# Neighbourhood attention layer on one core: where the sums of the output weights are formed, and in which order the first three row pairs are multiplied

## The chip, the cores and the metric

The kernel runs on one core of a Trainium2 chip. Its time is the device time of one execution in microseconds, and a kernel's number is the median of its runs. A trace comes from one further execution under the hardware profiler; it has its own time, which is given beside the span that the trace covers.

A core has five engines with a queue of instructions each, worked off in order: TensorE (PE; its weight loads are shown apart as PEld), VectorE (DVE), ScalarE (ACT), GpSimd (POOL) and SyncE (SP). They wait for each other through semaphores alone. SyncE issues almost all DMAs here. A DMA takes one of eight lanes in turn, and its issue waits until the DMA before it on the same lane, that is the eighth before it, has landed.

## The reference

One layer, in float32, on 2048 tokens of width 1024, seen as a grid of 32 rows by 64 columns with 16 heads of 64:

```python
def neighbourhood_mixer(h, w_in, rpb):
    B, S, _ = h.shape
    proj = h @ w_in
    q, k, v, gate = jnp.split(proj, 4, axis=-1)
    heads = lambda a: a.reshape(B, S, N_HEADS, HEAD_DIM)
    o = neighbourhood_attention(heads(q), heads(k), heads(v), rpb)
    return o.reshape(B, S, D_INNER), gate

def reference(x, norm_0, w_in_0, rpb_0, w_out_0, norm_1, w_in_1, w_out_1, norm_f):
    layers = ((norm_0, w_in_0, rpb_0, w_out_0), (norm_1, w_in_1, None, w_out_1))
    for i in range(DEPTH):
        g, w_in, rpb, w_out = layers[i]
        h = rmsnorm(x, g)
...
            o, gate = neighbourhood_mixer(h, w_in, rpb)
...
        x = x + (o * jax.nn.silu(gate)) @ w_out
    return rmsnorm(x, norm_f)
```

`DEPTH` is 1. Each query attends to a window of 8 rows by 16 columns with a bias per head. The part that the change touches is the last product, `(o * silu(gate)) @ w_out`, with `w_out` of 1024 x 1024, and the residual and the norm behind it.

## The kernel before, in words

**Precision.** Every large product is made in a format of reduced precision (fp32r). A float32 operand is split into a high part (a copy by ACT) and a low part (DVE subtracts the high part from the operand), and a product is three matmuls: high by high, low by high, high by low. `split_to` (L508 on) and `form_rows` (L1408) do this.

**Seven products.** Two halves in each of the three dimensions would take eight block products; a scheme with sums takes seven. At the end of the kernel one such unit is a pair of row tiles of 128 tokens. The left operand A is the gated attention output of the pair (A11, A12 of the first tile, A21, A22 of the second), the right one, B, is `w_out` in four quarters B11, B12, B21, B22 of 512 x 512, each four blocks of 128 x 512 with an index k. The products are P1 = A11 B11, P2 = A12 B21, P3 = S4 B22, P4 = A22 T4, P5 = S1 T1, P6 = S2 T2, P7 = S3 T3. S1 to S4 are sums of A (`sum_rows`), and the sums of B are T1 = B12 - B11, T3 = B22 - B12, T2 = B22 - T1 and T4 = B21 - T2; each is written over one of its operands, T1 over B11, T3 over B12, T2 over B22 and T4 over B21. A product is 12 matmuls of 128 x 128 by 128 x 512: four k by three of the split. P2 adds into the bank of P1 after P1's result was copied (`p1`, by ACT), P7 and P4 into that of P6, P3 into that of P5.

**Stages.** `stage_one` (to about 322 us) makes 12 units of the input projection and half of the values by seven products. `stage_two` (L799) finishes V: `pair(u, ts, ...)` (L889 to L902) multiplies V tiles of 24 or 48 matmuls, and puts a step of other work (its later arguments) behind every quarter of them. These steps make V's eviction (`v`, ACT, L392, and its store, L395), load and split V's weights (`lw`, L531, and `w`, L540 and L543), form the sums of the inputs (`t123`, `t4`, L863 to L871) and split them (`form`, `t1`, L518 and L519), and form the first operands of the projections that follow (`ahead`, L418, L419, sums L425). Then `run` makes these projections; the first product starts at 411.30 us in the trace. There the copy of P1 is L444, and P2 is its third product.

**Attention.** 32 cycles follow, one for each pair of heads and quarter of the rows, with scores (L1028), a softmax whose normalising of `x` is shared by DVE, ACT and GpSimd (L1054, L1056), transposes (`ph`, L1113), copies of these by DVE and ACT (`pta`, L1089) and values (`o`, L1135). Projections, and later the plain output products of the first six row tiles (L1337 to L1341), are fed between. The gated output goes to DRAM (`ogd`, L1144).

**The end.** `rows_by_seven` (L1465) multiplies the other ten row tiles as five pairs. The quarters of `w_out` are loaded in the last two cycles (`land_first`, 11 blocks; `land_rest`, 5 blocks), GpSimd forms T1 (`sum_T1`, L1374) and T2 and T3 (`sums_T23`, L1378 and L1379), DVE forms T4 (`sum_T4`, L1383), and `split_quarter` (L1394 by ACT, L1395 by DVE) splits all 16 blocks into the places that have come free by then. B11, B21 and B22 themselves lie split in `woh` and `wol` from the plain output products. The order of the products (`seq`) is P1 of the first three pairs, P2 of the first three pairs, and then 6, 7, 5, 4, 3 of the first pair, of the second and of the third, and after that each of the last two pairs in the order 1, 6, 2, 7, 5, 4, 3. `todo` hangs the other steps on places of this list: a product's operand is formed three products ahead (`form_rows`), and the loads and sums of rows and the residual's loads stand at fixed distances.

**Order.** Nothing is scheduled by a program: every engine works in the order in which the code calls it. `store(key, lag, f)` puts a DMA on a list, and `due(n)` issues what has become due after `lag` further matmuls; the DMA still takes its place in SyncE's one queue, and waits there for its data and its lane while everything behind it waits too.

Of the kernel before, what the change touches and what calls it, by code (L numbers as in the profile page):

```python
# [32 lines left out]
PLAIN = 6  # L33
# [38 lines left out]
def build(ctx, tc, x, xr, xt, wg, rpb, last, w_out, n0, nf, masks, out):  # L72
# [7 lines left out]
    ogd = [dram.tile([128, 4, NP, 128], F32, name=f"ogd{T}") for T in range(4)]  # L80

# [75 lines left out]
    woh, wol = {}, {}  # L157

# [640 lines left out]
    def stage_two():  # L799
# [81 lines left out]

        def t1(*ks):
            def g():
                for k in ks:
                    split_to(*X2["B12"][k], x12[k], None)
                X2["T1"] = X2["B12"]
            return g

        pair(0, (8, 9), both(w(0, 3), lambda: spread_rstd(3)), both(lw(1, 0), block("B12", x12, 0, 1)), block("B12", x12, 2, 3),  # L889
             block("B22", x22, 0, 1))  # L890
        pair(0, (10, 11), both(v(0, 8, 9), block("B22", x22, 2, 3)), t123(0), t123(1), lw(1, 1))
        pair(0, (12, 13), v(0, 10, 11), t123(2), t123(3), both(t4(0, 1, 2, 3), lw(1, 2)))
        pair(0, (14, 15), both(v(0, 12, 13), w(1, 0)), both(w(1, 1), lw(1, 3)), w(1, 2), w(1, 3))
        pair(1, (12,), v(0, 14, 15), form("T2", x11, 0), form("T2", x11, 1))
        pair(1, (13,), both(v(1, 12), form("T2", x11, 2)), form("T2", x11, 3))
        pair(1, (14,), both(v(1, 13), form("T3", x22, 0)), form("T3", x22, 1))
        pair(1, (15,), both(v(1, 14), lambda: ahead(-9, -1)), form("T3", x22, 2), form("T3", x22, 3))
        pair(1, (8,), both(v(1, 15), lambda: ahead(-8, -1)), t1(0), t1(1), lambda: ahead(-7, -1))
        pair(1, (9,), both(v(1, 8), t1(2)), t1(3), lambda: ahead(-6, -1), form("T4", x21, 0))
        pair(1, (10,), both(v(1, 9), form("T4", x21, 1)), form("T4", x21, 2), form("T4", x21, 3))  # L900
        pair(1, (11,), both(v(1, 10), lambda: ahead(-5)), lambda: ahead(-4), both(lambda: ahead(-3), lambda: ahead(-2)),
             both(lambda: ahead(-1), v(1, 11)))  # L902
# [451 lines left out]
    quarters = {"B11": (0, 0), "B12": (0, 1), "B21": (1, 0), "B22": (1, 1)}  # L1354

    def load_quarter(f, k, to):
        r, c = quarters[f]
        R[f, k] = to
        nc.sync.dma_start(to, w_out[(4 * r + k) * 128:(4 * r + k + 1) * 128, c * 512:c * 512 + 512])

    def land_first():
        spot = mkp([128, 3, 512], F32, "land")
        homes = [spot[:, i] for i in range(3)] + [kp([128, 960], F32, "land")[:, :512]]
        homes += [mp([128, 512], F32, "land") for _ in range(4)] + [p([128, 512], F32, "land") for p in (qp, sp, lp)]
        which = [(f, k) for f in ("B12", "B11") for k in range(4)] + [("B22", k) for k in range(3)]
        return [lambda w=w, h=h: load_quarter(*w, h) for w, h in zip(which, homes)]

    def land_rest():
        for w in [("B22", 3)] + [("B21", k) for k in range(4)]:
            load_quarter(*w, mp([128, 512], F32, "land"))  # L1370

    def sum_T1():
        for k in range(4):
            nc.gpsimd.tensor_tensor(R["B11", k], R["B12", k], R["B11", k], OP.subtract)  # L1374

    def sums_T23(ks):
        for k in ks:
            nc.gpsimd.tensor_tensor(R["B12", k], R["B22", k], R["B12", k], OP.subtract)  # L1378
            nc.gpsimd.tensor_tensor(R["B22", k], R["B22", k], R["B11", k], OP.subtract)  # L1379

    def sum_T4():
        for k in range(4):
            nc.vector.tensor_tensor(R["B21", k], R["B21", k], R["B22", k], OP.subtract)  # L1383

# [3 lines left out]
    def split_quarter(f, homes):  # L1388
        src = {"T1": "B11", "T2": "B22", "T3": "B12", "T4": "B21"}[f]
        TF[f] = []  # L1390
        for k in range(4):
            h, l = homes.pop(0), homes.pop(0)
            t, h, l = R[src, k], h() if callable(h) else h, l() if callable(l) else l
            nc.scalar.activation(h, t, AF.Copy)  # L1394
            nc.vector.tensor_tensor(l, t, h.bitcast(F32), OP.subtract)  # L1395
            TF[f].append((h, l))

    def fresh(p, n=512):
        return lambda: p([128, n], F32R, "t")[:, :512]

    def load_rows_of(m, f):
# [3 lines left out]
        A[m, f] = raw([128, 512], F32, "raw")  # L1405
# [59 lines left out]
    def rows_by_seven():  # L1465
        for f, (r, c) in plain_of.items():
            TF[f] = [(woh[4 * r + k, c], wol[4 * r + k, c]) for k in range(4)]
        E = 3 if PLAIN <= 6 else 2
        seq = [(m, P) for P in (1, 2) for m in range(E)] + [(m, P) for m in range(E) for P in order7 if P not in (1, 2)]
        seq += [(m, P) for m in range(E, len(PAIRS)) for P in order7]  # L1470
        at = {s: i for i, s in enumerate(seq)}
# [4 lines left out]

        for i, s in enumerate(seq):
            if i >= 2 * E:
                on(i - 3, form_rows, *s)
        for m in range(len(PAIRS)):  # L1480
            s = at[m, 6] - (m >= E)
            loads = {0: (), 1: ((-7, "A21"), (-6, "A22")), 2: ((-7, "A21"), (-6, "A22"), (-6, "A11"), (-6, "A12"))}
            for d, f in loads.get(m, ((-7, "A21"), (-7, "A22"), (-6, "A11"), (-4, "A12"))):
                on(s + d, load_rows_of, m, f)
# [5 lines left out]
        for f in ("A21", "A22"):  # L1490
            load_rows_of(0, f)
# [217 lines left out]
```

## Time and profile before

| | us |
|---|---|
| runs, median (lowest, highest) | 1065.47 (1064.48, 1067.84) |
| profiled execution, its own time | 1068.24 |
| span of its trace | 1066.5 |
| TensorE busy in the span | 1044.3 |

| stretch | what runs |
|---|---|
| 0 to 322 | stage one |
| 324 to 411 | V tiles of stage two |
| 411 to 936 | projections, attention, plain output products |
| 936 to 948 | transposes and values of the last cycle |
| 948 to 1060 | 35 products of the five pairs |
| 1060 to 1066.5 | last row's norm and store |

The trace is read in views: the page (busy time of each engine, groups of instructions), windows (busy time of each engine in a stretch), waits (which engine waited for which instruction: total, times, longest), the timeline (start, duration, engine, line, names of tiles, number of instructions run together; in brackets the idle time before it and what ended it), and the chain of waits that ended last. L12 is line 12 of the kernel before. A number such as 128x512 is partitions by elements of a tile.

### The profile page before, as it was taken

The page shows a single profiled execution, that of the slowest core. Times are in us where ns is not written, and L with a number is a line of the kernel's source. Part 1 is how long each engine was busy: PE and PEld are TensorE (multiplying, and loading weights), DVE is VectorE, ACT ScalarE, POOL GpSimd, SP SyncE. Part 2 cuts the span into 40 slices and gives each one's busy share as a digit, 9 for nine tenths or more (in the row PEclk, how much of TensorE's full clock was granted, in tenths as well). Part 3 has the DMA queues.
Part 4 walks back from the last instruction along what each step waited for, and adds up shares of the span by engine and source line. Part 5 has one row for each costly group of instructions (what it writes and reads, how often), then busy time and mean ns, then how long its engine had stood idle before and what let it go on. Part 6 is the DMA issues. An engine that isn't in the chain of part 4 may idle for free.

```text
span 1066.5 us, 20216 instructions
## 1 busy us (share of the span) xinstructions
PE 1044.3 (98%) x7256; PEld 852.9 (80%) x7256; DVE 742.4 (70%) x1589; ACT 558.4 (52%) x1305; POOL 297.4 (28%) x369
## 2 busy tenths in 40 slices
PE   9999999999999999999999999999999999988897
PEld 6888888887888888888888788888877778866686
DVE  5476657778897635465655766678787887778886
ACT  7645233533344334232333677788888777744333
POOL 0000322312221000000002576656556223361231
PEclk9999999999999999999999999999999999988999
DMA  9634444444545334333326878788885798964452
GB/s 315 218 99 121 131 143 138 126 132 142 174 135 148 113 89 108 109 102 121 103 89 226 246 224 246 208 249 272 242 262 186 221 333 258 323 212 126 141 178 80
DMA packets 124285, 189.05 MB, mean 177 GB/s; under 512 B 11224, under 2 KB 55512, under 8 KB 124184
## 3 DMA queue, kind: packets, MB, share of 16 engines
q1 hardware_dynamic: 123752, 187.35, 56.1%
q8 instruction: 57, 0.93, 0.3%
q10 hardware_dynamic: 432, 0.40, 0.1%
q14 instruction: 44, 0.36, 0.1%
HBM read 137.38 MB, written 50.33 MB: 176 GB/s over the span
## 4 chain that ended last, share of the span: by engine, by line
PE 87%; DVE 6%; DMA 2%; ACT 2%; issue 1%; POOL 1%; SPq 0%; ACTq 0%; DVEq 0%; POOLq 0%
PE pp L436 36%; PE pv L560 16%; PE s L1028 7%; PE o L1135 7%; PE py L1437 7%; PE ph L1113 4%; PE pp L382 2%; PE po L1337 2%; PE pp L384 2%; PE po L1339 2%; PE pp L380 2%; PE po L1341 2%; DMA land<-in_w_out_dram 1%; DVE f L1412 1%; DMA q<-qd 1%
## 5 line engine op out<-in xcount | busy, mean ns | idle before, releaser
L436 PE MATMUL pp<-h,f 128*128 128x512 f32 x672 | 217.4, 389 | 0.0
L1042 ACT ACTIVATE x<-x,st 128x360 f32<-128x360 f32 (+5 forms) x256 | 151.2, 593 | 24.4 <-DVE st L1036 24.4
L436 PEld LDWEIGHTS pp<-h,f 128*128 128x128 f32 x672 | 126.1, 188 | 26.1
L436 PE MATMUL pp<-t,f 128*128 128x512 f32 x558 | 141.7, 389 | 0.1
L1056 POOL TENSOR_SCALAR x<-x,st 128x480 f32<-128x480 f32 (+5 forms) x192 | 115.9, 622 | 86.1 <-DVE st L1047 84.2
L456 POOL TENSOR_TENSOR tmp<-tmp,rb 128x512 f32<-128x512 f32 x36 | 58.4, 1623 | 268.9 <-DVE tmp L454 233.4
L436 PE MATMUL pp<-l,f 128*128 128x512 f32 x336 | 130.7, 389 | 0.0
L996 POOL TENSOR_TENSOR em<-e,mk 128x264 f32<-128x264 f32 (+3 forms) x64 | 50.9, 826 | 260.1 <-DMA mk<-in_masks_dram 246.7
L1036 DVE CUSTOM_DVE_ANT_0 x<-s,em 128x360 f32<-128x360 f32 (+5 forms) x256 | 123.0, 535 | 0.1
L436 PEld LDWEIGHTS pp<-t,f 128*128 128x128 f32 x558 | 104.7, 188 | 22.3 <-DVE u L449 0.6
L419 DVE TENSOR_TENSOR f<-raw,f 128x512 fp32r<-128x512 f32 x105 | 76.5, 729 | 43.6 <-ACT f L418 43.5
L1028 PE MATMUL s<-kt,q 64*128 64x480 f32 (+5 forms) x512 | 95.7, 487 | 0.2
L1135 PEld LDWEIGHTS o<-pta,vt 120*64 120x64 f32 (+2 forms) x1792 | 82.8, 140 | 13.9 <-DVE st L1036 13.6
L560 PE MATMUL pv<-wh,h 128*128 128x512 f32 x256 | 88.8, 392 | 0.2 <-ACT wh L540 0.2
L560 PE MATMUL pv<-wh,l 128*128 128x512 f32 x256 | 88.2, 389 | 0.0
L560 PE MATMUL pv<-wl,h 128*128 128x512 f32 x256 | 88.1, 389 | 0.0
L1135 PE MATMUL o<-pta,vt 120*64 120x128 f32 (+5 forms) x1792 | 87.4, 256 | 0.0
L1028 PEld LDWEIGHTS s<-kt,q 64*128 64x128 f32 x512 | 64.8, 186 | 16.8 <-DVE pta L1089 2.1
L418 ACT ACTIVATE f<-raw 128x512 fp32r<-128x512 f32 x105 | 63.7, 624 | 26.5 <-PE pp L436 12.5
L1089 DVE COPY pta<-ph 120x512 f32<-120x512 f32 (+5 forms) x96 | 56.9, 639 | 25.3 <-PE ph L1113 25.1
L436 PEld LDWEIGHTS pp<-l,f 128*128 128x128 f32 x336 | 63.1, 188 | 13.2
L1089 ACT ACTIVATE pta<-ph 120x512 f32<-120x512 f32 (+5 forms) x96 | 49.6, 557 | 37.1 <-PE ph L1113 36.4
(193 smaller groups left out, 1882.1 us busy)
## 6 DMA issues: line engine op xcount, KB each, us to landing
raw<-in_wg_dram SPq DMA_DIRECT2D x124, 256.0 KB, 4.4
row<-in_xr_dram SPq DMA_DIRECT2D x32, 256.0 KB, 4.0
vd<-v SPq DMA_DIRECT2D x32, 256.0 KB, 2.5
sgd<-sg SPq DMA_DIRECT2D x32, 256.0 KB, 2.4
q<-qd SPq DMA_DIRECT2D x32, 256.0 KB, 5.4
sgt<-sgd SPq DMA_DIRECT2D x32, 256.0 KB, 5.9
xr<-in_x_dram SPq DMA_DIRECT2D x32, 256.0 KB, 3.6
ogd<-og SPq DMA_DIRECT2D x32, 256.0 KB, 4.0
```

Of the source, the lines that this page charges most:

```text
L418: nc.scalar.activation(t[:, 0], src, AF.Copy)
L419: nc.vector.tensor_tensor(t[:, 1], src, t[:, 0].bitcast(F32), OP.subtract)
L436: nc.tensor.matmul(B[n, P], t[:, int(m == 2), c], x[k][int(m == 1)], start=P in (1, 6, 5) and k == 0 and m == 0, stop=k == 3 and m == 2, s ...
L456: nc.gpsimd.tensor_tensor(tmp, tmp, rb[c], OP.mult)
L560: nc.tensor.matmul(ps[t], a[:, o], b, start=k == 0 and m == 0, stop=k == NK - 1 and m == 2)
L1028: nc.tensor.matmul(pst[s], qt[a, qs], kt[a, :r1 - r0, c0:c1].rearrange("p r (s c) -> p s r c", c=8), start=True, stop=True)
L1036: nc.vector.tensor_tensor_reduce(X[i, C][s], pst[s], EM[p, ROW_TYPE[T], COL_TYPE[C], s], -1.0, 1e38, OP.add, OP.min, st[:, o:o + 1])
L1042: nc.scalar.activation(X[i, C][s], X[i, C][s], AF.Exp, bias=st[:, o:o + 1], scale=-1.0, accum_out=st[:, 4 + o:5 + o])
L1056: nc.gpsimd.tensor_scalar(X[i, C][s], X[i, C][s], st[:, o:o + 1], 1.0, op0=OP.mult, op1=OP.mult)
L1089: (nc.vector.tensor_copy if h else lambda o, i_: nc.scalar.activation(o, i_, AF.Copy))(t[:k, h, b * 512:b * 512 + w], banks_[b, h][:k, :w])
L1135: nc.tensor.matmul(to.rearrange("d (h q) -> d h q", q=64) if nq > 64 else to, vt[:k, strip, s * 64:s * 64 + 64], t[:k, h, at:at + 64] if n ...
L1437: nc.tensor.matmul(B[m, P], t[:, a, c], b, start=P in (1, 6, 5) and k == 0 and i == 0, stop=k == 3 and i == 2, skip_group_check=True)
```

## The change

The 16 sums T1 to T4 (four blocks each) are formed in stage two. `out_rows(k)` loads the four blocks of row k of `w_out`, `out_sum(k, f)` subtracts, splits the result, and stores both parts to a new DRAM tensor `wod`. At the end the parts are loaded as they are, 32 loads of 256 KB (`land`), in place of 16 loads, 16 sums and 16 splits. T2's eight parts go to places of `woh` and `wol` that the plain output products have used for the last time. Four buffers of stage two hold the loaded blocks (two of `ep`, two of `kp`), so the loads of the next k stand behind the last sum of the one before.

The products of the first three pairs behind P1 and P2 are interleaved, and their operands are formed four products ahead; loads and sums of rows have new places in `todo`, and the row loads A21 and A22 of the first pair go out with `land_rest`, into `vh`.

```diff
+    wod = {f: dram.tile([128, 4, 2, 512], F32, name=f"wod{f}") for f in ("T1", "T2", "T3", "T4")}
...
+        def out_rows(k):
+            def g():
+                for q, (r_, c_) in quarters.items():
+                    OW[q] = kp([128, 960], F32, "ow")[:, :512] if r_ else ep([128, 512], F32, "ow")
+                    nc.sync.dma_start(OW[q], w_out[(4 * r_ + k) * 128:(4 * r_ + k + 1) * 128, c_ * 512:c_ * 512 + 512])
+            return g
+
+        def out_sum(k, f):
+            def g():
+                a, b = {"T1": ("B12", "B11"), "T3": ("B22", "B12"), "T2": ("B22", "B11"), "T4": ("B21", "B22")}[f]
+                o = OW[{"T1": "B11", "T3": "B12", "T2": "B22", "T4": "B21"}[f]]
+                nc.vector.tensor_tensor(o, OW[a], OW[b], OP.subtract)
+                h, l = ev([128, 512], F32R, "oh"), ev([128, 512], F32R, "ol")
+                split_to(h, l, o, None)
+                for i, s in enumerate((h, l)):
+                    store(("ow", f, k, i), 5, lambda i=i, s=s: nc.sync.dma_start(wod[f][:, k, i], s.bitcast(F32)))
+            return g
...
-        pair(0, (14, 15), both(v(0, 12, 13), w(1, 0)), both(w(1, 1), lw(1, 3)), w(1, 2), w(1, 3))
-        pair(1, (12,), v(0, 14, 15), form("T2", x11, 0), form("T2", x11, 1))
-        pair(1, (13,), both(v(1, 12), form("T2", x11, 2)), form("T2", x11, 3))
+        pair(0, (8, 9), both(w(0, 3), lambda: spread_rstd(3)), both(lw(1, 0), block("B12", x12, 0, 1)),
+             both(block("B12", x12, 2, 3), out_rows(0)), block("B22", x22, 0, 1))
+        pair(0, (10, 11), both(v(0, 8, 9), block("B22", x22, 2, 3)), t123(0), t123(1), both(lw(1, 1), out_sum(0, "T1")))
+        pair(0, (12, 13), both(v(0, 10, 11), out_sum(0, "T3")), t123(2), t123(3), both(t4(0, 1, 2, 3), lw(1, 2)))
+        pair(0, (14, 15), both(v(0, 12, 13), w(1, 0), out_sum(0, "T2")), both(w(1, 1), lw(1, 3)), both(w(1, 2), out_sum(0, "T4")),
+             both(w(1, 3), out_rows(1)))
+        pair(1, (12,), v(0, 14, 15), form("T2", x11, 0), form("T2", x11, 1), out_sum(1, "T1"))
+        pair(1, (13,), both(v(1, 12), form("T2", x11, 2)), form("T2", x11, 3), out_sum(1, "T3"), out_sum(1, "T2"))
+        pair(1, (14,), both(v(1, 13), form("T3", x22, 0)), form("T3", x22, 1), out_sum(1, "T4"), out_rows(2))
+        pair(1, (15,), both(v(1, 14), lambda: ahead(-9, -1)), form("T3", x22, 2), form("T3", x22, 3), out_sum(2, "T1"))
+        pair(1, (8,), both(v(1, 15), lambda: ahead(-8, -1)), both(t1(0), out_sum(2, "T3")), t1(1), both(lambda: ahead(-7, -1), out_sum(2, "T2")))
+        pair(1, (9,), both(v(1, 8), t1(2)), both(t1(3), out_sum(2, "T4")), both(lambda: ahead(-6, -1), out_rows(3)), form("T4", x21, 0))
+        pair(1, (10,), both(v(1, 9), form("T4", x21, 1)), form("T4", x21, 2), both(form("T4", x21, 3), out_sum(3, "T1")), out_sum(3, "T3"))
+        pair(1, (11,), both(v(1, 10), lambda: ahead(-5)), both(lambda: ahead(-4), out_sum(3, "T2")), both(lambda: ahead(-3), lambda: ahead(-2)),
+             both(lambda: ahead(-1), v(1, 11), out_sum(3, "T4")))
...
+    def land(where, homes):
+        for (f, k, i), h in zip(where, homes):
+            TF.setdefault(f, [[None, None] for _ in range(4)])[k][i] = h
+            nc.sync.dma_start(h.bitcast(F32), wod[f][:, k, i])
+
+    parts7 = [(f, k, i) for f in ("T3", "T1", "T4") for k in range(4) for i in range(2)]
+
+    def land_first():
+        spot = mkp([128, 3, 512], F32R, "t")
+        land(parts7[:10], [spot[:, i] for i in range(3)] + [kp([128, 960], F32R, "t")[:, :512]] +
+             [mp([128, 512], F32R, "t") for _ in range(4)] + [p([128, 512], F32R, "t") for p in (sp, lp)])
+
+    def land_rest():
+        land(parts7[10:17], [kp([128, 960], F32R, "t")[:, :512]] + [mp([128, 512], F32R, "t") for _ in range(6)])
+        for f in ("A21", "A22"):
+            load_rows_of(0, f, vh)
+
+    def land_T2():
+        land([("T2", k, i) for k in range(4) for i in range(2)], [a[k, 1] for k in range(4) for a in (woh, wol)])
+
+    def land_T4():
+        land(parts7[17:], sixths() + [sp([128, 512], F32R, "t")])
...
-        E = 3 if PLAIN <= 6 else 2
-        seq = [(m, P) for P in (1, 2) for m in range(E)] + [(m, P) for m in range(E) for P in order7 if P not in (1, 2)]
+        E, LEAD = 3, 4
+        seq = [(m, P) for P in (1, 2) for m in range(E)]
+        seq += [(0, 6), (1, 6), (0, 7), (0, 5), (1, 7), (0, 4), (1, 5), (0, 3), (1, 4), (2, 6), (1, 3), (2, 7), (2, 5), (2, 4), (2, 3)]
...
         for i, s in enumerate(seq):
             if i >= 2 * E:
-                on(i - 3, form_rows, *s)
+                on(i - (LEAD if i < seq.index((E, 1)) else 3), form_rows, *s)
...
-        split_quarter("T2", [a[k, 1] for k in range(4) for a in (woh, wol)])
-        sixth = sixths()
+        land_T4()
         for i, (m, P) in enumerate(seq):
             rows_product(m, P)
-            if i == 0:
-                sum_T4()
-                split_quarter("T3", [fresh(lp)] + [fresh(vh)] * 2 + [fresh(sp)] + sixth[:4])
-            if i == 3:
-                spot = mkp([128, 3, 512], F32R, "t1")
-                split_quarter("T1", [spot[:, j] for j in range(3)] + [fresh(kp, 960)] + sixth[4:6] + [fresh(vh)] * 2)
-            if i == 5:
-                split_quarter("T4", [fresh(mp)] * 6 + [fresh(kp, 960), fresh(mp)])
...
         if m == cycles:
             all_loads()
             feed(6)
+            while next(outs, 0) != 0:
+                due(1)
+            land_T2()
...
-            if m == cycles - 1:
-                sum_T1()
...
-        if m == cycles - 1:
-            sums_T23((0,))
```

In the last cycle the 12 sums of GpSimd and their calls go, and what was left of the plain output products is now issued behind `feed(6)`, ahead of `land_T2`. Over the whole kernel TensorE and ACT have as many instructions as before; DVE has 12 more, GpSimd 12 fewer, and SyncE has 62 more DMAs: 16 loads and 32 stores in stage two, 32 loads of parts in place of 16 of quarters at the end, and two loads of rows fewer (A11 and A12 of the third pair were loaded a second time for its sums).

88 lines of the change are left out of this document (25 added, 63 removed).

## The prediction

> **What bounds the kernel now.** I read the page's busy times first, then windows around the two places that the change touches, then TensorE's waits in the last fifth.
>
> ```profile
> span 1066.5 us, 20216 instructions
> PE 1044.3 (98%) x7256; PEld 852.9 (80%) x7256; DVE 742.4 (70%) x1589; ACT 558.4 (52%) x1305; POOL 297.4 (28%) x369
> 348.00:411.00 63.00, 63.00 (x279) 52.16 (x279) 29.56 (x47) 22.13 (x41) 0.00 (x0) 1.00 0.34 98
> 948.00:1021.00 73.00, 63.56 (x261) 49.85 (x258) 63.48 (x103) 28.21 (x61) 18.02 (x11) 0.93 0.46 144
> 1021.00:1060.00 39.00, 38.95 (x171) 31.64 (x169) 30.89 (x56) 14.67 (x37) 9.51 (x6) 1.00 0.28 95
> ```
>
> The columns of a window are: stretch, PE, PEld, DVE, ACT, POOL busy, granted clock, DMA share, GB/s. TensorE is the bound: whatever delays it anywhere moves the end by as much, and what DVE, ACT, GpSimd and the queues do is free until TensorE waits for it. In stage two (348 to 411) it never waits, and DVE is idle for 33 us of the 63. From 948 to 1021, the first 21 products of the end, it is idle for 9.4 us and runs partly at a lower clock; the later products lose nothing.
>
> ```profile
> PE py L1437 <- ACT f L1411: 4.5, 2, 2.6
> PE ph L1113 <- POOL x L1056: 4.2, 2, 4.0
> PE py L1437 <- DVE u L1447: 3.5, 1, 3.5
> PE py L1437 <- DVE f L1412: 1.2, 1, 1.2
> 929.35 2.67 PE L1135 MATMUL o<-pta,vt 96*64 96x128 f32 x56
> ...
> 941.75 0.34 PE L1113 MATMUL ph<-ident,x 64*96 64x64 f32 x2 [4.02 <-POOL x L1056]
> ...
> 943.65 4.80 PE L1135 MATMUL o<-pta,vt 96*64 96x128 f32 x56
> 948.37 0.50 PE L1437 MATMUL py<-woh,f 128*128 128x512 f32 x1
> 973.21 2.90 PE L1437 MATMUL py<-t,f 128*128 128x512 f32 x6 [3.50 <-DVE u L1447]
> ...
> 992.50 2.90 PE L1437 MATMUL py<-t,f 128*128 128x512 f32 x6 [2.62 <-ACT f L1411]
> ...
> 1010.15 1.63 PE L1437 MATMUL py<-t,f 128*128 128x512 f32 x6 [1.91 <-ACT f L1411]
> 1037.96 22.04 PE py L1437 x96
> ```
>
> The first four lines are waits (total, times, longest); the rest are stretches of TensorE. Its idle times of 4.02, 3.50 and 2.62 us are each followed by matmuls at about half speed (4.80 against 2.67 us for 56, 2.90 against 1.63 for six); 1.91 us idle is not.
>
> **End: the 21 products.** TensorE's instructions are the same, only their order is new. At full clock and with no wait 96 matmuls take 22.04 us, so a product of 12 takes 2.755, and 21 take 57.9. The chain of TensorE ends at 1060.0; the 14 products of the last two pairs take 38.6 of it, so the 21 last from 948.4 to 1021.4, which is 73.0 us. If none waits, 15.1 us are gained: 9.4 of idle time, the rest half speed and restarts. Would they wait? The DVE was their queue, and this is what is taken off it:
>
> ```profile
> L1395 DVE TENSOR_TENSOR t<-land,t 128x512 fp32r<-128x512 f32 x9 | 5.8, 684 | 0.2 <-ACT t L1394 0.2
> L1395 DVE TENSOR_TENSOR wol<-land,woh 128x512 fp32r<-128x512 f32 x4 | 3.0, 804 | 0.0
> L1383 DVE TENSOR_TENSOR land<-land 128x512 f32<-128x512 f32 x4 | 2.5, 686 | 0.0
> L1395 DVE TENSOR_TENSOR sixths<-land,sixths 128x512 fp32r<-128x512 f32 x3 | 2.0, 685 | 0.0
> ```
>
> That is 13.3 us of 63.5, so 50.2 us of DVE work stand in 57.9 us. Walking DVE's new order against TensorE's, every form (now four products ahead) is done at least 3 us before its product. The landings: 32 of 256 KB in place of 16. T2's first product stands seventh, 16.5 us after the first; T4's twelfth, 30 us after. The DMA is busy for 0.46 of this stretch, and a landing issued around 946 has 10 us or more to spare, even with the 6.7 us of the rows below. I take 15.1; at worst two of the three long waits stay in another place, about 7.
>
> **End: the wait for GpSimd in the last cycle.**
>
> ```profile
> 929.09 5.02 POOL L1374 TENSOR_TENSOR land<-land 128x512 f32<-128x512 f32 x4 [5.51 <-DMA land<-in_w_out_dram]
> 934.09 2.99 POOL L1056 TENSOR_SCALAR x<-x,st 128x288 f32<-128x288 f32 x4
> ...
> 940.16 2.10 POOL L1056 TENSOR_SCALAR x<-x,st 128x384 f32<-128x384 f32 x2
> 938.94 1.15 ACT L1411 ACTIVATE f<-raw 128x512 fp32r<-128x512 f32 x2 [0.61 <-DMA raw<-ogd]
> DMA to landing us min/median/max: 6.5/6.7/6.7
> ```
>
> GpSimd's normalising (L1056) stood behind T1's sums, which waited for their loads, and behind two more sums. With the 12 sums gone it can be done by about 936, and the 4.02 us go. What is late next: on ACT and DVE the three forms of A11 (L1411, L1412) stand ahead of the copies of `pta`, and they wait for rows that take 6.7 us to land. One load fewer ahead of them brings these rows forward by about 0.6 us. So `o`'s first copy comes at about 940.9 and its last at 942; TensorE has then idled some 2.7 us, about what halved the clock above, and `o` ends at 946.4 instead of 948.4: 2.0 gained. Bounds: 0 (the rows as late as TensorE now is), 3.9 (same copies, full clock), 6.1 (all 4.02 us and the 2.1 of half speed). The forms keep it near the low side. The end gains 17.1.
>
> **Stage two: 16 loads, 16 sums, 32 stores.** A sum is a subtract, ACT's copy, a subtract. Its price is that of the same chain, here with L514 in the place of the first subtract:
>
> ```profile
> 331.05 0.75 DVE L514 SCALAR_TENSOR_TENSOR land<-land,g,rb 128x512 f32<-128x512 f32 x1
> 332.50 0.69 DVE L519 TENSOR_TENSOR l<-land,h 128x512 fp32r<-128x512 f32 x1 [0.70 <-ACT h L518]
> 333.11 0.74 DVE L514 SCALAR_TENSOR_TENSOR land<-land,g,rb 128x512 f32<-128x512 f32 x1
> L543 DVE TENSOR_TENSOR wl<-raw,wh 128x512 fp32r<-128x512 f32 x8 | 5.2, 690 | 6.1 <-ACT wh L540 6.1
> 365.47 1.29 DVE L543 TENSOR_TENSOR wl<-raw,wh 128x512 fp32r<-128x512 f32 x2 [1.43 <-ACT wh L540]
> DMA to landing us min/median/max: 3.3/4.4/4.6
> 411.30 0.39 PE L436 MATMUL pp<-h,f 128*128 128x512 f32 x1
> ...
> 416.74 0.39 PE L436 MATMUL pp<-h,f 128*128 128x512 f32 x1
> 414.22 0.60 ACT L444 ACTIVATE p<-pp 128x512 f32<-128x512 f32 x1 [2.12 <-PE pp L436]
> ```
>
> 333.11 less 331.05 is 2.06 us a sum, on an engine that works in order: 16 take 33 us, as much as DVE has idle. But the four loads of round k+1 go into the buffers of round k and stand behind T4(k)'s stores on the queue of SyncE, so each round opens with a landing in which the sums, and all that stands behind them on DVE, wait. With 4.4 us (the L413 loads' median here) and two issues before it, about 5.4 per round. In round 0 T1, T3 and T2 (6.2 us) go into 4.7 of the 6.1 us that DVE now waits in front of L543; T4(0) follows the split that ends at 366.8, so it is done at 366.8 + 1.1 + 2.06, about 369.9. A round is then 5.4 + 4 x 2.06 + five splits of 0.61 (their spacing) and about 0.9 of waits for ACT's copies, 17.5. T4(1) ends at 387.4, T4(2) at 404.9, and round 3 lands at 410.3. Behind its T1 and T3 on DVE stand the forms of the first projection, so the product that TensorE starts at 411.3 starts near 415.9.
>
> The longer delay is behind it. P1's copy (L444), without which the third product (416.74) may not add into the same bank, stands on ACT behind T4(3)'s copy, and that on DVE behind three sums and eight forms and row sums: 410.3 + 6.2 + 4.9 + 0.6, then two ACT steps of 0.6, gives 423.2, and the third product starts at 423.7 in place of 416.74. That is 7.0 lost; the 4.6 us of waiting before it are among the 7. Idle times of this length halved the clock: one slow six, 2.90 less 1.63, 1.3 more. Before that, V's last weights come about 1 us late (their loads now stand behind stores), and this is absorbed in the same wait. Nothing later gives it back, since TensorE is busy to the end. Loss 8.3. Bounds: landings of 3.3 in three rounds bring all of it 3.3 us forward and spare the slow clock in part, so 3.7; the 6.7 of the last cycle's rows, 2.3 more in each of three rounds, 15.2. The DMA share here is 0.34 (0.83 and more where 6.7 was seen), so I keep 4.4.
>
> Two rules of the Trainium skill bear on this. DMA: Bandwidth & Descriptors (Anatomy of one DMA) has about 2.0 us fixed plus bytes over 436 GB/s, by which 256 KB would take an estimated 2.6 us and the loss would be 5.4 less; the trace's 4.4 median disagrees and is used. TensorE: Matmul & The Clock Gate (What's actually happening) has the clock halve after an idle window of about 3.4 us, on a free-running counter; by it the 2.7 us before `o` need not halve the clock and the sum would gain 1.9 more, while the trace halves it after 2.62.
>
> **Sum.** 8.3 lost and 17.1 gained: 8.8 less. The profiled execution took 1068.24 (span 1066.5 and 1.7 around it) and would take 1059.4; it lies 2.8 over the median of the runs, 1065.47, from which 1056.7 follows.
>
> **Rivals.**
> Stage two nearly hidden: the landings take 3.3, loss 3.7, time 1052.1. For it: 33 us of idle DVE time, no other traffic. Against: 4.4 as median at the same place. Chance 0.18.
>
> The last cycle's wait wholly gone: 6.1 in place of 2.0, time 1052.6. For it: GpSimd is the named releaser. Against: the forms' order on ACT and DVE. Chance 0.08.
>
> The end stays bound by DVE, or T2 and T4 land late: 7 of the 15.1, time 1064.8. For it: DVE is 87% filled even then, and 16 more landings. Against: the slack above, and the last two pairs, with the same DVE work per product, which lose nothing. That the interleaving doesn't remove the waits is this case too. Chance 0.13.
>
> Slower: SyncE's queue is strictly in order, and between the sums' stores stand V's stores, which wait for a V tile of 24 matmuls (279 take 63 us, so 5.4). If a round's end slips past such a store, the next round's loads go out one tile later, and with them the sums and V's evictions behind these. Three rounds of 5.4 make 16.2 on top of 8.3: 24.5 lost, 1072.9. It decides from 8.8 us of extra loss on, that is from the second slip, which alone ends at 1067.5. For it: this row.
>
> ```profile
> SPq L395 <- ACT v L392: 48.9, 10, 7.9
> ```
>
> Against: in my walk those stores are issued some 8 us before the loads behind them. Chance 0.10, 0.02 of it for two slips.
>
> **How the numbers follow.** The forecast has 0.51, with its own range 1052 to 1061. A measurement of this kernel tells about 0.3%, 3.2 us, from no change. Below 1062.3 lie the first two rivals, nearly all of the forecast and a little of the third: 0.79 faster. The rest of the third, the tail of the forecast and the two slips: 0.13 the same. The slower case: 0.08. The range from 1050 to 1065 reaches to the third rival and leaves out the slower one and the joint luck of the first two.
>
> **What would show it.** Right: no wait of TensorE over 1 us in the products of the first three pairs, 21 products in 58 us; `ph` no longer waits for POOL, but `o` waits for a `pta` copy; in stage two three gaps of about 5 us on DVE ended by a landing of `ow`, TensorE waiting near 411 and 417 for some 7 us together, first for a form, then for P1's copy. Wrong: TensorE busy through 411 to 425 (first rival), DVE waits in the products (third), or stage two's first projection later than 430 (slower).

## The result and the profile after

| | before | after |
|---|---|---|
| median of 7 runs (lowest, highest), us | 1066.13 (1062.98, 1069.36) | 1060.39 (1058.1, 1063.76) |
| profiled execution, its own time | 1068.24 | 1060.0 |
| span of its trace | 1066.5 | 1058.2 |

After by before is 0.9948, with a 95% interval of 0.9927 to 0.9969: 5.7 us less (3.3 to 7.8 by the interval), inside the stated range, and less than the forecast of 8.8. The page after, then a few of its windows (stretch, PE, PEld, DVE, ACT, POOL busy, granted clock, DMA share, GB/s) and all of TensorE's waits (total, times, longest):

```profile
span 1058.2 us, 20319 instructions
PE 1040.5 (98%) x7256; PEld 850.9 (80%) x7256; DVE 743.7 (70%) x1601; ACT 557.9 (53%) x1305; POOL 279.2 (26%) x357
```

```profile
348.00:411.00 63.00, 61.48 (x271) 50.31 (x270) 43.37 (x69) 26.90 (x49) 0.00 (x0) 1.00 0.72 233
952.50:1013.70 61.20, 58.92 (x255) 48.20 (x254) 47.83 (x83) 21.21 (x49) 14.94 (x9) 0.98 0.62 215
```

```profile
PE pp L438 <- ACT p L446: 2.8, 1, 2.8
PE o L1158 <- ACT pta L1112: 2.4, 1, 2.4
PE py L1439 <- DVE y L1236: 2.3, 1, 2.3
PE pv L562 <- ACT wh L542: 2.0, 2, 1.2
PE zp L126 <- DVE z L123: 1.2, 1, 1.2
PE o L1158 <- DVE pta L1112: 0.4, 1, 0.4
PE pv L562 <- DVE wl L545: 0.3, 1, 0.3
```

The waits of before from the last cycle on are gone. In their place stand others: for V's last weights (L562) and at a projection's product (L438) in stage two, before `o` (L1158) in the last cycle, and one in the products (L1439). In stage two DVE is busy for 43.4 us of the 63 where it was 29.6; in the 21 products it is busy for 47.8 in 61.2, where it was 63.5 in 73.0.

Since TensorE's instructions are the same up to the order of the products, the two traces can be laid over each other matmul by matmul. The distance between them changes at these places, and by 0.2 in all the others together:

| place | distance changes by, us |
|---|---|
| the first 20 matmuls | +2.0 |
| stage two, to the third product of the projections | +5.1 |
| from the last cycle's second half of `ph` to the first product (11.63, now 8.85) | -2.8 |
| the 21 products (73.1, now 61.2) | -11.9 |
| the last 14 products up to the start of the last matmul (38.15, now 38.17) | 0.0 |
| behind the last product | -0.5 |

The first row isn't the change's. These are the starts of the two traces, before and after; the columns are start, duration, engine, line and names, with the idle time ahead in brackets:

```profile
4.98 1.18 PE L560 MATMUL pv<-wh,h 128*128 128x512 f32 x2 [0.20 <-ACT wh L540]
```

```profile
5.56 1.22 PE L562 MATMUL pv<-wh,h 128*128 128x512 f32 x2 [0.78 <-ACT wh L542]
```

The first weights came 0.6 us later in the second one, and the clock stayed low for longer: the trace's record of the granted clock has full speed from 9.71 us on, that of before from 5.98 on, and 0.6 us late becomes 2.0 by the 21st matmul. Late weights alone don't do it: in e7 (below) they come 0.4 late, at 5.36, but the full clock is granted from 4.11 on, and nothing is lost. Of the profiled executions of this study, five of the fourteen show this late start, a kernel with the stage two of before among them, and the others start within 0.7 us of before's. Below, 'lost in stage two' is always counted behind this start. Without it the two profiled executions are 10.3 us apart, and the medians 5.7: before's profiled execution lay 2.1 above its median and after's 0.4 below. What made the former long stays open, since only one execution of before was profiled. Nine more runs of before, taken beside e10, go from 1064.51 us at a mean granted clock of 0.996 to 1067.47 at 0.989, so how often the clock is lowered may be a part of it.

### The profile page after: what moved, and what is told of

Its sections match the earlier page's. It is cut to its first block, busy times and chain, and to the rows that moved or that the text cites. A ratio compares the mean times of both kernels' runs of the same rounds, so it can differ in the third digit from the quotient of the medians.

```text
span 1058.2 us, 20319 instructions
## 1 busy us (share of the span) xinstructions
PE 1040.5 (98%) x7256; PEld 850.9 (80%) x7256; DVE 743.7 (70%) x1601; ACT 557.9 (53%) x1305; POOL 279.2 (26%) x357
## 4 chain that ended last, share of the span: by engine, by line
PE 55%; DMA 2%; DVE 1%; ACT 1%; issue 1%; SPq 0%; DVEq 0%; ACTq 0%
PE pp L438 16%; PE py L1439 9%; PE s L1051 8%; PE o L1158 7%; PE ph L1136 4%; PE pp L384 2%; PE pp L386 2%; PE pp L382 2%; PE po L1360 2%; PE po L1362 2%; PE po L1364 2%; DMA t<-wodT 1%; DMA raw<-ogd 1%; DMA em<-in_last_dram 0%; DVE x L1059 0%
## 5 line engine op out<-in xcount | busy, mean ns | idle before, releaser
L438 PE MATMUL pp<-h,f 128*128 128x512 f32 x672 | 217.8, 389 | 2.8 <-ACT p L446 2.8
L438 PEld LDWEIGHTS pp<-h,f 128*128 128x128 f32 x672 | 126.0, 188 | 29.5 <-ACT p L446 3.2
L438 PE MATMUL pp<-t,f 128*128 128x512 f32 x558 | 141.8, 389 | 0.1
L438 PE MATMUL pp<-l,f 128*128 128x512 f32 x336 | 130.7, 389 | 0.0
L438 PEld LDWEIGHTS pp<-t,f 128*128 128x128 f32 x558 | 104.6, 188 | 22.5 <-DVE u L451 0.9
L1158 PEld LDWEIGHTS o<-pta,vt 120*64 120x64 f32 (+2 forms) x1792 | 82.7, 140 | 16.6 <-DVE st L1059 13.6
L562 PE MATMUL pv<-wh,h 128*128 128x512 f32 x256 | 89.3, 394 | 2.0 <-ACT wh L542 2.0
L1158 PE MATMUL o<-pta,vt 120*64 120x128 f32 (+5 forms) x1792 | 87.4, 256 | 2.7 <-ACT pta L1112 2.4
L562 PE MATMUL pv<-wl,h 128*128 128x512 f32 x256 | 89.0, 393 | 0.3 <-DVE wl L545 0.3
L562 PE MATMUL pv<-wh,l 128*128 128x512 f32 x256 | 88.6, 391 | 0.0
L438 PEld LDWEIGHTS pp<-l,f 128*128 128x128 f32 x336 | 63.1, 188 | 13.1
```

The lines of the kernel that those rows point to most:

```text
L438: nc.tensor.matmul(B[n, P], t[:, int(m == 2), c], x[k][int(m == 1)], start=P in (1, 6, 5) and k == 0 and m == 0, stop=k == 3 and m == 2, s ...
L562: nc.tensor.matmul(ps[t], a[:, o], b, start=k == 0 and m == 0, stop=k == NK - 1 and m == 2)
L1158: nc.tensor.matmul(to.rearrange("d (h q) -> d h q", q=64) if nq > 64 else to, vt[:k, strip, s * 64:s * 64 + 64], t[:k, h, at:at + 64] if n ...
```

## The experiments

All times of single runs below are one execution, and the runs from e1 on were made on three chips, so whole times compare less well than stretches, which come from the traces. The two that decide most are the stretch of the 21 products and the loss in stage two, which is counted up to the third product of the projections. Stretches with the same code tell what a difference means: the loss in stage two is 5.1 to 6.1 us in seven runs, `ph` to the first product takes 7.2 to 9.1 in ten, and the 21 products take 60.5 to 61.5 in five.

| run | time | lost in stage two | from `ph` to the first product | 21 products |
|---|---|---|---|---|
| before, profiled | 1068.24 | 0 | 11.6 | 73.1 |
| after, profiled | 1060.0 | 5.1 | 8.9 | 61.2 |
| e1_old_order | 1062.88 | 6.1 | 8.0 | 66.3 |
| e2_new_order_only | 1068.03 | -0.1 | 11.9 | 70.5 |
| e3_no_sums | 1054.15 | -0.1 | 8.5 | 60.9 |
| e4_late_sums | 1055.69 | 3.5 | 9.1 | 60.5 |
| e5_early_weights | 1056.38 | 6.4 | 7.2 | 60.7 |
| e7_copies_first | 1054.94 | 5.6 | 4.7 | 62.1 |
| e8_p5_earlier | 1062.59 | 5.3 | 8.0 | 63.0 |
| e9_old_order_lead4 | 1065.12 | 5.5 | 8.8 | 68.4 |
| e10_rolling_loads | 1057.79 | 4.9 | 8.1 | 61.5 |
| e13_lag | 1057.52 | 5.5 | 7.8 | 59.2 |
| e14_old_order_lag | 1064.65 | 5.7 | 8.7 | 66.3 |
| e12_together (median of 5; profiled 1048.96) | 1047.49 | 0.1 | 4.7 | 58.3 |

In e13 and e14 half speed behind the third product takes some 1.4 us more, which this column doesn't have.

### What made the products faster: DVE freed, or their order?

e1_old_order puts the old order back on the kernel after; forms are three products ahead again, and the loads and sums of rows go back to fixed distances from each pair's P6 (not shown):

```diff
-        seq += [(0, 6), (1, 6), (0, 7), (0, 5), (1, 7), (0, 4), (1, 5), (0, 3), (1, 4), (2, 6), (1, 3), (2, 7), (2, 5), (2, 4), (2, 3)]
+        seq += [(m, P) for m in range(E) for P in order7 if P not in (1, 2)]
```

> The sums stay in stage two, the products of the first three pairs go back to each pair in turn, forms three products ahead. The 21 products of the first three pairs took 73.0 us before and 61.0 after. Theory 'DVE freed': the 13.3 us of splits taken off DVE made the gain, the order little: 58 to 62 us, time within 1.5 us of after. Rival 'order': the interleaving made it: 68 us or more, time 7 us or more above after.

e2_new_order_only puts the new order on the kernel before, with new places for the loads and sums of rows (not shown) and forms three products ahead:

```diff
-        seq = [(m, P) for P in (1, 2) for m in range(E)] + [(m, P) for m in range(E) for P in order7 if P not in (1, 2)]
+        seq = [(m, P) for P in (1, 2) for m in range(E)]
+        seq += [(0, 6), (1, 6), (0, 7), (0, 5), (1, 7), (0, 4), (1, 5), (0, 3), (1, 4), (2, 6), (1, 3), (2, 7), (2, 5), (2, 4), (2, 3)]
```

> The kernel before with the new order of products alone; sums and splits stay at the end (forms three ahead, and the rows' loads stand where the old buffers allow them). Theory 'DVE freed': 68 us or more for the 21 products, no more than 5 of the 73.0 gained. Rival 'order': 62 or less.

In this run P6 of the first pair takes S4, since S4 is written over S2 before the form. Measured: 66.3 and 70.5. Of the 11.9 us the sums out of the way give 6.8 with the old order, the order gives 2.6 with the sums in place, and together they give 2.5 more than the two; the forms four products ahead are in these 2.5. The windows of e1 and e2 (columns as above):

```profile
950.00:1016.50 66.50, 60.84 (x258) 48.30 (x255) 49.54 (x82) 21.50 (x49) 14.86 (x9) 0.97 0.59 209
950.70:1021.20 70.50, 62.62 (x255) 49.63 (x254) 60.54 (x104) 28.15 (x62) 17.57 (x11) 0.94 0.46 145
```

TensorE's idle time, which leaves out what the lower clock costs, is 9.4 us in before, 5.7 in e1, 7.9 in e2 and 2.3 in after: 3.7 less by the sums, 1.5 by the order, 1.9 more by both. So e1 fell between the theories: DVE's relief is the larger part, and the order is far from little. TensorE's waits in e1:

```profile
PE py L1439 <- ACT f L1413: 4.5, 2, 2.6
...
PE py L1439 <- DVE u L1449: 0.9, 1, 0.9
```

The wait of 3.50 for DVE has shrunk to 0.9. The two for a form on ACT, 2.62 and 1.91, are those of before to the hundredth. The sums and splits at the end aren't their cause. This is what ACT does in e1 just before the second of them ends, at 1005.23:

```profile
1001.84 0.63 ACT L1239 ACTIVATE u<-y 128x512 f32<-128x512 f32 x1 [0.51 <-DVE y L1236]
...
1003.89 0.20 ACT L1259 ACTIVATE st<-st 128x1 f32<-128x1 f32 x1 [1.32 <-DVE st L1258]
1004.00 0.61 ACT L1413 ACTIVATE f<-raw 128x512 fp32r<-128x512 f32 x1
1004.52 0.61 ACT L1413 ACTIVATE f<-s 128x512 fp32r<-128x512 f32 x1
1005.04 0.62 ACT L1413 ACTIVATE f<-raw 128x512 fp32r<-128x512 f32 x1
```

Forms stand behind the root of a finished tile (L1259), whose input DVE makes behind the scaling of the tile before it (L1279). Two experiments try to move them apart within the old order: e9 forms one product earlier, e14 scales 12 matmuls later.

```diff
-        E, LEAD = 3, 3
+        E, LEAD = 3, 4
```

> As e1_old_order (sums in stage two, each pair in turn: 66.3 us for the 21 products, with waits of 2.62 and 1.91 before P7 of the second and the third pair), but forms four products ahead. Theory 'distance': the two waits go, 62 or less. Rival 'order': the forms still stand behind the finishing of the pair before on ACT and DVE, 65 or more.

```diff
-            store(("y", n), 12 if n == tiles - 2 else 24, scale)
-            store(("y", n), 44, send)
+            store(("y", n), 12 if n == tiles - 2 else 36 if n < 12 else 24, scale)
+            store(("y", n), 50 if n < 12 else 44, send)
```

> As e1_old_order (sums in stage two, each pair in turn; 66.3 us for the 21 products, of it waits of 2.62 and 1.91 before P7 of the second and third pair, while a form stands on ACT behind a root whose input stands on DVE behind a finished tile's scaling), with the scaling of the first six finished tiles 12 matmuls later. Theory 'finishing work in the way': the two waits shrink by the 1.4 us of a scaling each, or go: 64 or less. Rival 'only the order of products': they stay, 66.

e9 made it worse, 68.4, so the theory 'distance' falls: the waits are 3.55 and 2.85 now, the first of them for DVE's sum of P6 (L1449). Forms called earlier stand ahead of other work that a product needs; that this is the reason was not tried by itself. In e14 the mechanism shows and the gain does not:

```profile
PE py L1439 <- DVE y L1236: 2.7, 2, 1.4
PE py L1439 <- ACT f L1413: 2.5, 2, 1.6
```

The two waits for forms shrank by 1.0 us each, and two of 1.4 came up before P3 of the same pairs: the scaling now stands ahead of P5's sum (L1236), which must have read the bank before P3 adds to it. Total unchanged, 66.3. My reading, which no run tests by itself: a pair has more of this work within its last five products than they cover, and it needs products of another pair between, which is what the interleaving gives.

### The last wait of the products

After's only wait in the 21 products is of the same kind. DVE ahead of the 21st product:

```profile
1006.04 1.67 DVE L1420 TENSOR_TENSOR s<-s,raw 128x512 f32<-128x512 f32 x1
1007.63 2.44 DVE L1279 SCALAR_TENSOR_TENSOR y<-y,st,acc 128x512 f32<-128x512 f32 x2
1009.99 0.68 DVE L1236 TENSOR_TENSOR y<-py,u 128x512 f32<-128x512 f32 x1
```

```profile
1010.82 0.47 PE L1439 MATMUL py<-woh,f 128*128 128x512 f32 x1 [2.28 <-DVE y L1236]
```

P5's sum of the third pair stands behind a row sum and a scaling that are long while GpSimd works, from 1005.54 to 1008.85 (1.67 and 2.44, against 0.69 and 1.41 at 955.62 and 956.83, where it is idle). e8 moves P5 of the third pair ahead of P3 of the second; e13 is the later scaling of e14 on the kernel after.

```diff
-(1, 4), (2, 6), (1, 3), (2, 7), (2, 5), (2, 4), (2, 3)]
+(1, 4), (2, 6), (2, 7), (2, 5), (1, 3), (2, 4), (2, 3)]
```

> P5 of the third pair is moved ahead of P3 of the second, so that two products lie between P5 and P3 of the third pair. Theory: the wait of 2.28 us before the 21st product (its bank is read by P5's sum, which stands on DVE behind a finished tile's scaling) goes; 21 products in about 59 in place of 61.2. Rival: DVE is short of time there and the wait moves to another product: 61.

> After with the scaling of the first six finished tiles (two DVE instructions, 2.4 us beside GpSimd) 12 matmuls later. Theory: P5's sum of the third pair is no longer behind a scaling, the wait of 2.28 us before the 21st product goes, 21 products in 59. Rival 'DVE is full there': the wait moves to a later product, also among the last 14, which took 38.2 with no wait so far.

```profile
PE py L1439 <- ACT f L1413: 2.2, 1, 2.2
PE py L1439 <- DVE y L1236: 0.8, 1, 0.8
```

The first line is e8's, the second e13's. In e8 a wait of 2.2 us moved to P7 of the third pair, now for its form, and half speed followed it: 63.0, and the rival holds. In e13 it went, 59.2 although its first product ran at the lower clock and took 2.0 more than at full speed; but 0.85 came up later, among the last 14 (39.0 in place of 38.2; 38.9 in e8). Both theories are partly right: about 2 us gained here, 0.8 given back.

### The last cycle

e7 calls the forms of A11 behind the transposes and their copies:

```diff
-        if m == cycles:
-            for n in range(3 if PLAIN <= 6 else 2):
-                form_rows(n, 1)
...
         if m == cycles:
+            for n in range(3):
+                form_rows(n, 1)
             all_loads()
```

> The forms of the three A11 are called behind the last transposes' copies on ACT and DVE. Theory: the wait of 2.4 and 0.4 us before the last cycle's o shrinks to about 1.2, too short to lower the clock, and o takes 2.7 again: from the first ph of the last half to the first product 6 to 7 us in place of 8.2, and the first product at full speed, 3 to 4 us less than after. Rival: the forms are late in turn and the wait moves to the first products: less than 1 us.

TensorE in after, then in e7:

```profile
947.43 0.66 PE L1158 MATMUL o<-pta,vt 96*64 96x128 f32 x8 [2.37 <-ACT pta L1112]
948.44 4.11 PE L1158 MATMUL o<-pta,vt 96*64 96x64 f32 x48 [0.36 <-DVE pta L1112]
```

```profile
943.35 0.66 PE L1158 MATMUL o<-pta,vt 96*64 96x128 f32 x8
944.40 2.23 PE L1158 MATMUL o<-pta,vt 96*64 96x64 f32 x48 [0.40 <-DVE pta L1112]
```

The 48 matmuls of `o` take 2.23 in place of 4.11, and from `ph` to the first product it is 4.7 in place of 8.9; that product takes 2.85 in place of 4.11. That is 4.1 and 1.3 us, somewhat more than expected, and no form is late. Against the ten runs with after's last cycle (7.2 to 9.1, first product 2.87 to 4.75) it is 2.5 to 4.4 and 0 to 1.9, since the clock falls differently in each. From before's 11.6 to 4.7 it is 6.9, more than the 6.1 of the rival 'the last cycle's wait wholly gone': that rival was open in the hardware, and shut by the order of calls alone.

### Stage two

e3 leaves out the loads and the arithmetic of the sums, and the 32 stores send parts that exist already:

```diff
+                return
                 for q, (r_, c_) in quarters.items():
...
-                nc.vector.tensor_tensor(o, OW[a], OW[b], OP.subtract)
-                h, l = ev([128, 512], F32R, "oh"), ev([128, 512], F32R, "ol")
-                split_to(h, l, o, None)
+                h, l = X2["B11"][k]
```

> The kernel after without the 16 loads and the arithmetic of the 16 sums in stage two; the 32 stores stay and store parts that exist already (what they store is not the sums). Theory 'order of work on DVE and ACT': both waits of stage two go, the 1.5 us before V's last weights and the 2.75 us before the third product; 5.0 us less than after. Rival 'stores': the wait for V's weights stays, since their loads still stand behind stores in SyncE's queue; 3 us less.

```profile
348.00:411.00 63.00, 63.00 (x279) 52.18 (x278) 29.00 (x46) 22.14 (x41) 0.00 (x0) 1.00 0.64 215
```

In e3 TensorE is busy for the whole window, and no wait is left in stage two. The 32 stores cost nothing when their data are ready; the whole loss is that of the loads and sums, and of what stands in SyncE's queue behind a store that waits for its sum. e4 calls the last two sums behind the first products, e5 lets V's last weights load ahead of T2(0)'s stores, e10 loads each block of the next k as soon as its buffer is free, and its calls of `out_rows(1)` to `out_rows(3)` between the V tiles go.

```diff
+            if n == 1 - len(units_two) and i in (0, 1):
+                out_sum(3, ("T2", "T4")[i])()
...
-        pair(1, (11,), both(v(1, 10), lambda: ahead(-5)), both(lambda: ahead(-4), out_sum(3, "T2")), both(lambda: ahead(-3), lambda: ahead(-2)),
-             both(lambda: ahead(-1), v(1, 11), out_sum(3, "T4")))
+        pair(1, (11,), both(v(1, 10), lambda: ahead(-5)), lambda: ahead(-4), both(lambda: ahead(-3), lambda: ahead(-2)),
+             both(lambda: ahead(-1), v(1, 11)))
```

> The last two sums, T2 and T4 of k = 3, are called behind the first and the second product of the projections, so behind P1's copy on ACT. Theory: the 2.75 us before the third product go, nothing takes their place; 3.0 us less than after. Rival: a form behind the sums on DVE is late by as much, and the wait moves to the next product: within 1 us of after.

```diff
-        pair(0, (14, 15), both(v(0, 12, 13), w(1, 0), out_sum(0, "T2")), both(w(1, 1), lw(1, 3)), both(w(1, 2), out_sum(0, "T4")),
+        pair(0, (14, 15), both(v(0, 12, 13), w(1, 0)), both(w(1, 1), lw(1, 3)), both(w(1, 2), out_sum(0, "T2"), out_sum(0, "T4")),
```

> T2(0) is called one step of two V quarters later, so the loads of V's last weights stand ahead of its stores in SyncE's queue. Theory 'chain': the 1.2 us (and 0.3) before these weights go, but the third product of the projections is set by the chain of landings, sums and P1's copy, so its wait of 2.75 grows by as much: within 1 us of after, once the first microseconds of the run are taken out. Rival 'sum of waits': 1.5 us less than after.

```diff
-                for q, (r_, c_) in quarters.items():
+                for q in qs:
+                    r_, c_ = quarters[q]
...
+                if k < 3:
+                    out_rows(k + 1, {"T1": (), "T3": ("B12",), "T2": ("B11",), "T4": ("B21", "B22")}[f])()
```

> Stage two alone: a block of the next k is loaded as soon as its buffer is free (B12 behind T3, B11 behind T2, the other two behind T4) in place of all four behind T4. Theory 'landings in the chain': DVE's waits for ow go, the sums end some 8 us earlier, P1's copy is no longer late and the 2.75 us before the third product go; what stays of the 5 to 6 us lost in stage two is the wait before V's last weights, 1 to 2 us. Rival: DVE's own work sets the chain, the landings only fill its idle time; 1 us gained at most.

TensorE in e5, then TensorE's waits in stage two in e10:

```profile
413.81 0.50 PE L438 MATMUL pp<-h,f 128*128 128x512 f32 x1 [2.78 <-ACT f L420]
422.58 0.50 PE L438 MATMUL pp<-h,f 128*128 128x512 f32 x1 [1.19 <-ACT p L446]
```

```profile
PE pv L562 <- ACT wh L542: 2.4, 1, 2.4
...
PE pv L562 <- DVE wl L545: 0.4, 2, 0.3
```

In e4 the wait before the third product went, and one of 1.29 us for the first form came up: 3.5 lost, some 2 us better than the seven runs with after's stage two (5.1 to 6.1), between theory and rival. In e5 the wait for V's weights went, and the loss stayed, 6.4: the late weights had been covered by the chain behind them. In e10 DVE no longer waits for a landing of `ow`, and nothing waits at the third product; but the early loads stand ahead of V's last weights, which now come 2.4 us late, and half speed behind that takes 1.7 more: 4.9 lost. So the chain changed as the theory had it, and the gain was that of the rival. Each of the two edits alone gains 1 us or nothing, since each leaves the other's delay in place. With both, in e12, the loss is 0.1 up to the third product and 0.4 at 458 us.

### Together

> Rolling loads, V's last weights ahead of T2(0), the last cycle's copies ahead of the forms, and the later scaling together. Theory: stage two loses 1 us or less in place of 5 to 6, from ph to the first product 4.7 in place of 8.0 to 8.9, 21 products in 58 to 59: 9 to 11 us under after, 1049 to 1052. Rival: one wait gives way to the next, 1054 or more.

It has the edits of e5, e7, e10 and e13. 1047.49 as a median of five runs (1045.57 to 1048.96): 0.9822 of before, interval 0.9808 to 0.9836, and 12.9 us under the median of after (the two medians of before beside them are 0.4 apart); slightly better than expected. TensorE's waits over the whole of it:

```profile
PE zp L126 <- DVE z L123: 1.2, 1, 1.2
PE py L1442 <- DVE y L1239: 0.9, 1, 0.9
PE pv L562 <- ACT wh L542: 0.8, 1, 0.8
PE py L1442 <- DVE u L1452: 0.6, 1, 0.6
PE o L1161 <- DVE pta L1115: 0.4, 1, 0.4
PE s L1054 <- ACT k L368: 0.3, 1, 0.3
```

## Why the prediction was right, and where its terms were off

Direction, range and the three places hold. The forecast had 17.1 gained at the end and 8.3 lost in stage two; the traces have 14.7 (2.8 and 11.9) and 5.1. Both are some 3 us (2.4 and 3.2) too large, and that they cancel is luck: the traces without the start give 10.3 less, against 8.8, of which 0.5 lies behind the last product. That the medians give 5.7 is not explained by a term of the sum, as said above.

**The 21 products, 15.1.** The step 'every form is done at least 3 us before its product' held (4.9 us or more in after), and it was too narrow: a product also waits for the bank that it adds to. P5's sum behind a scaling gave the wait of 2.28. The floor of 57.9 was some 0.7 long itself: an undisturbed product of after starts 2.72 behind the one before it, 57.1 for 21. The rest of the difference is the first product, at a low clock (4.11 against 2.87 before); it is the price of the wait before `o`, which I had put into the last cycle, and it isn't a fixed one: in the ten runs with this last cycle the first product takes 2.87 to 4.75. And what I took for one cause were two: of the 11.9 DVE's relief alone gives 6.8, the order alone 2.6, and both 2.5 more.

**T2 and T4's landings.** No wait for a DMA in the products. Right.

**The last cycle, 2.0.** GpSimd's wait went, and `o` waited 2.37 and 0.36 for copies behind forms that waited for rows, at a low clock, as the walk had it. 2.8 gained less 1.2 in the first product is 1.6.

**Stage two, 8.3.** The chain was right: after's DVE waits for the landings of `ow`, and the third product for P1's copy behind T4(3):

```profile
DVE ow L897 <- DMA ow<-in_w_out_dram: 4.8, 2, 3.4
```

```profile
423.80 0.50 PE L438 MATMUL pp<-h,f 128*128 128x512 f32 x1 [2.75 <-ACT p L446]
```

The walk had 423.7 for this product, and 423.80 was measured, but in an execution whose start was 2.0 late, so the walk was some 2 us long, and that the two figures agree is luck. Two landings held DVE up by 3.4 and 1.4 us in place of three by about 5, since splits of V's and of the inputs' sums fill part of a landing; the last round's first block landed in 3.2. And the 1.3 for a low clock did not come in after: 2.75 us idle, and the next 12 matmuls take 2.91. In e13 and e14 it came, behind the same wait: 4.44 and 4.29 for 12, some 1.4 more. The term holds in some executions and not in others. The step 'V's last weights come late and this is absorbed in the same wait' held: in e5 they come in time, and the loss is 6.4, not less than the 5.1 to 6.1 of the seven. The 4.6 us of waiting before the first product were not seen in after, where TensorE was late itself; e5 shows 2.78 of them.

Landings of `ow`, over the last three rounds, which settles the first of the two rules weighed:

```profile
DMA to landing us min/median/max: 3.2/4.4/5.0
```

The median is the one taken, 4.4, and the shortest, 3.2, is over the 2.6 us estimated from the Trainium skill (DMA: Bandwidth & Descriptors, Anatomy of one DMA). That section gives its fit for DMAs issued by GpSimd, and these are issued by SyncE, so it was no rule for this place.

**The rivals.** Stage two hidden: no, 5.1. The wait wholly gone: no, and possible (e7). DVE bound at the end: in one place, 2.3 us in place of the 8 that this rival had. Slower: V's stores between the sums' did not hold a round back; the loads of the three rounds (372.19, 389.55 and 406.62 us) go out right behind T4's last stores (371.81, 389.18 and 406.25).

## What to carry to other kernels

When work is moved into a stretch where an engine is idle on average, the cost is in what stands behind it in order on that engine and on the DMA queue: here 20 us of idle DVE remained, and 5 us were lost to late loads and to one copy, nearly all of it recoverable by moving calls. Two late chains can cover each other, so that each fix alone gains nothing and both gain all; lay the traces over each other and fix both before judging either. A bank that the next product adds to is a wait like any operand: the sum that reads it must be ahead of work that nobody waits for.

## What the runs showed of the hardware

The clock does not go by the length of an idle time alone. 2.42 us idle in e10 are followed by matmuls at half speed; 2.62 us in e1, as long as a wait in before that was followed by half speed, are not:

```profile
374.76 0.50 PE L562 MATMUL pv<-wh,h 128*128 128x512 f32 x1 [2.42 <-ACT wh L542]
...
377.97 0.63 PE L562 MATMUL pv<-wh,l 128*128 128x512 f32 x1
```

```profile
989.12 3.23 PE L1439 MATMUL py<-t,f 128*128 128x512 f32 x13 [2.62 <-ACT f L1413]
```

A matmul alone takes 0.63 in the first (0.39 at full clock), and 13 take 3.23 in the second, full speed. The wait before the 21st product shows it on one place of the code: 2.28 us in after cost nothing more (the next 12 matmuls took 2.84), 2.25 us in e7 cost 1.6 (4.41).

The traces show what decides. Up to the last matmul the granted clock is 0.5 in stretches of 3.41 us, or two or three times that (e12 has none there), and within a trace these stretches begin whole multiples of 3.41 apart: in before at 941.23, 971.95 and 992.43, which is 9 and 6 times 3.41. So a trace can be cut into cells of 3.41 us by this grid. Here are two cells each around the wait for P1's copy, 2.77 us in e13 and 2.75 in after (stretch, PE, PEld, DVE, ACT, POOL busy, granted clock, DMA share, GB/s):

```profile
419.33:422.75 3.42, 0.65 (x3) 0.45 (x3) 2.37 (x4) 1.63 (x3) 0.00 (x0) 1.00 0.82 195
422.75:426.16 3.41, 3.41 (x10) 2.62 (x9) 2.72 (x5) 0.63 (x1) 0.00 (x0) 0.50 0.93 324
```

```profile
419.31:422.73 3.42, 1.73 (x8) 1.12 (x6) 3.24 (x6) 1.65 (x5) 0.00 (x0) 1.00 0.80 196
422.73:426.14 3.41, 2.34 (x10) 1.97 (x11) 2.16 (x4) 1.72 (x4) 0.00 (x0) 1.00 0.92 327
```

In e13 the wait lies in one cell, and the next has half the clock; in after it is split into 1.69 and 1.07, and neither is followed by half the clock. Over the fourteen traces, from 20 us to the last matmul, all 22 cells at full clock with 1.96 us or more of idle time are followed by half the clock, of the 11 with 1.49 to 1.94 us three are, and of those with less none is.

The Trainium skill (TensorE: Matmul & The Clock Gate, What's actually happening) has a counter that runs free of the kernel, which agrees with this; its idle time of about 3.4 us does not, since cells with 2 to 2.3 us of idle time were enough in many runs (e2, e7, e8 and e10 among them). So an idle time of 2 to 3 us has two prices, and which one is paid goes by where it falls on this grid, which lies differently in every run.
